# When a gated-convolution group is finished: two completions moved, and one priority kept for a single set of small matmuls

## The chip, the cores and the metric

The kernel runs on one core of a Trainium2 chip. The metric is the device time of one execution in microseconds. Of the kernel before three runs are known, with a median of 897.62 us (896.54 to 897.82). One more execution was profiled; it took 896.51 us, and the times in the tables and rows below are counted from the start of its span of 894.7 us.

The engines are TensorE (PE in the rows; its loads of stationary weights are PEld), VectorE (DVE), ScalarE (ACT), GpSimd (POOL) and SyncE (SP), which issues all DMAs of this kernel from one queue. Each engine works through its own queue in order, and waits where an operand or a buffer is not ready.

## The reference

One decoder layer over 2048 rows of width 1024, all in 32-bit floats, with 16 learned rows put in front:

```python
hn = rms_norm(h, norm_g)
proj = jnp.einsum('bld,de->ble', hn, w_in)
cx, cb, cc, cg, q, k, v, rg = jnp.split(proj, N_PROJ, axis=-1)

u = c_gate * h                        # cc * cx, then 3 causal taps per channel
conv_out = b_gate * conv(u) * jax.nn.silu(cg)

ret = head_group_norm(retention_chunkwise(rotary(q), rotary(k), v), ret_norm_g)
ret_out = ret * jax.nn.silu(rg)

mixed = jnp.concatenate([conv_out, ret_out], axis=-1)
h = h + jnp.einsum('ble,ed->bld', mixed, w_out)
return rms_norm(h, final_g)[:, N_META:]
```

There are four groups of 128 channels of the gated convolution, and four retention heads of 128 channels. A row's norm is a factor per row, so the kernel multiplies the raw x with the weights and scales afterwards: a tile `rr` holds that factor spread over the partitions, `rr2` its square.

## The kernel before, in words

**Two rounds, eight units each.** The rows are cut into two rounds of 1024. In each round eight units are worked through: four heads (units 0 to 3) and four convolution groups (units 4 to 7). `UNITS` (line 36) sets the order: round 0 starts with group 4, the opening group, then the four heads, then groups 5, 6, 7; round 1 takes the heads first and then groups 4 to 7, so that unit 7 is round 1's last group. After the rounds, eight pairs of output rows (2 x 128 rows each) are multiplied with `w_out`, added to x, normalised and stored (`output`, line 692).

**A quad.** The unit of matrix work is `quad` (line 201). It computes two 128-channel projections over 1024 rows as a 2 x 2 block product with seven block products instead of eight. Each block product is 12 matmuls of 128x128 weights by 128x512 columns: four steps over the inner dimension, times three, since each 32-bit operand is split into a rounded half (`wh`, `mh`, a cast on ScalarE, line 101) and a remainder (`wl`, `ml`, a subtraction on VectorE, line 113). So a quad is 84 matmuls, all of line 210. The sums and differences of weight blocks are made on GpSimd (`stationary`, lines 135 to 138), in place, over the blocks as they were loaded. Three buffers each of `wh` and `wl` are there, so the parts of a product can be made up to three products ahead. `quad_plain` (line 249) does the same with eight products from plain blocks (96 matmuls of line 260); the opening group's two quads, round 1's first, and the first pair of output rows use it. Results leave a PSUM bank through a function `take(i, j, bank, copy)`: projection i, half j of the rows.

A head has two quads (K and V, then Q and the gate), and behind them its retention: transposes, state updates, scores, normalisation (lines 616 to 687). A group has two quads as well: `cc` with `cx`, whose product is `u`, and `cg` with `cb`.

**What a group does besides.** `u` is scaled with `rr2`, `carry` (line 447) copies two columns from one half of the rows to the next, `taps` (line 453) makes the three taps (one ScalarE, two VectorE operations for each half). Then the gate `cg` is scaled with `rr` and goes through Silu, the taps are multiplied with `rr`, with the gate and with `cb`, and `store_mixed` (line 440) writes the half to a DRAM tensor `mixed`. There are four of these, one for each 512 rows, and the pairs of output rows read them: pairs 0 and 1 the first, pairs 2 and 3 the second, pairs 4 and 5 the third, pairs 6 and 7 the fourth. What round 1's last group stores is first read by pair 4.

In a normal group (`conv_group`, line 507) the taps come between the two quads, and the second quad's `take` multiplies straight into them (lines 536 to 547): the scaling of the gate on VectorE, Silu on ScalarE, two products on GpSimd, one on VectorE. The opening group (`group_plain`, line 462) copies its results out instead and returns a function `complete`, which does all of the above later. The main loop hands it to the next unit, head 0, as the first member of `between`; `head` (line 565) calls the first member behind its first quad and the second behind its second quad.

**Meta products.** In round 0 each unit's first weight blocks are also multiplied with the 16 learned rows: 32 small matmuls of line 395 (`meta_products`, line 388). They are issued from `ahead` (line 761), at the end of the unit before, and read the blocks as loaded; GpSimd's differences of `stationary`, which overwrite these blocks, wait for them. For the opening group they are issued at line 791, before its quads.

**What sets the order.** The kernel is written on top of a planner. The order of the program gives each instruction its priority; the planner goes through a modelled course of time, and puts into each engine's queue what is ready by its model, of what is ready the earliest in the program. So work of a later place can run before, where an engine is free. `tc.high_priority(offset=HIGH)`, with `HIGH = 400`, gives the instructions in its block the priority of a place 400 instructions earlier. Buffers come from pools with a set number for each tag: 16 of the general kind (`gen`, tag `g`: `u`, copies, taps, x, `w_out`, output rows), 8 raw weight blocks, 4 bank copies (tag `tc`), one rotation table (tag `rot_t`, 128 x 2048 floats).

Of the kernel before, what the change touches and what calls it, by code (L numbers as in the profile page):

```python
# [19 lines left out]
NG = 4  # L20
EPS = 1e-6
HB = 512
NR = 2
BLK = SEQ // NR
# [5 lines left out]
HIGH = 400  # L30
# [40 lines left out]
def hybrid_trunk(ctx: ExitStack, tc: tile.TileContext, t, out: bass.AP, chunk_decay):  # L71
# [5 lines left out]
    nc = tc.nc  # L77
# [307 lines left out]
        nc.vector.tensor_tensor(out=raw, in0=raw, in1=rows, op=ALU.mult)  # L385
        nc.vector.tensor_tensor(out=meta_s, in0=raw, in1=gains, op=ALU.mult)

    def meta_products(blocks):

        bank = ps_misc()  # L390
        four = [bank[i * 32 : i * 32 + NMETA, :P] for i in range(4)]
        with tc.high_priority(offset=HIGH):
            for kt in range(KH):
                for i in (3, 2, 1, 0):
                    nc.tensor.matmul(  # L395
                        four[i], meta_s[:, i % 2 * KH + kt, :], blocks[i][:, kt * P : (kt + 1) * P],
                        start=kt == 0, stop=kt == KH - 1,
                    )
# [41 lines left out]
    def store_mixed(r, j, kt, m):  # L440
        d = mixed[2 * r + j]
        nc.sync.dma_start(
            d[:, :, kt // KH, :, kt % KH, :].rearrange("a i p c -> p a i c"),
            m.rearrange("p (a i c) -> p a i c", a=2, i=2),
        )
# [7 lines left out]
    def taps(u, g):  # L453
        c = gen("c")[:, :HB]
        nc.scalar.mul(c, u[:, 2:], conv_w[:, g, 2:3])
        for tap in (1, 0):
            nc.vector.scalar_tensor_tensor(  # L457
                out=c, in0=u[:, tap : tap + HB], scalar=conv_w[:, g, tap : tap + 1], in1=c, op0=ALU.mult, op1=ALU.add
            )
        return c  # L460

    def group_plain(g, m, f, meta, first, between, ahead):


        u = [gen("u") for _ in range(2)]
        raws = []
        rr, rr2 = ([a[:, j * HB : (j + 1) * HB] for j in range(2)] for a in f[:2])

        def mul(eng, out, a, b):
            eng.tensor_tensor(out=out, in0=a, in1=b, op=ALU.mult)  # L470

        def take(i, j, pp, c):
            s = u[j][:, 2:]
            if i == 0:
                nc.scalar.copy(out=s, in_=pp)
            else:
                mul(nc.vector, s, pp, s)

        quad_plain(first[0], m, take)
        meta_carry(g, meta)  # L480

        def take(i, j, pp, c):
            c = gen("cb")[:, :HB]
            nc.scalar.copy(out=c, in_=pp)
            raws.append(c)

        quad_plain(first[1], m, take)
        between()
        blocks = ahead()

        def complete():
            for j in range(2):
                mul(nc.vector, u[j][:, 2:], u[j][:, 2:], rr2[j])
            carry(u, g, 0)
            for j in range(2):
                gate, other = raws[2 * j : 2 * j + 2]
                c = taps(u[j], g)
                mul(nc.vector, gate, gate, rr[j])
                nc.scalar.activation(gate, gate, AF.Silu)
                mul(nc.gpsimd, c, c, rr[j])  # L500
                mul(nc.vector, c, c, gate)
                mul(nc.vector, c, c, other)
                store_mixed(0, j, g, c)

        return blocks, complete

    def conv_group(g, r, m, f, blocks, ahead):
# [21 lines left out]
        blocks, meta = blocks  # L529
        quad(stationary(blocks), m, take)  # L530
        if meta:
            meta_carry(g, meta)
        carry(u, g, r)
        cs = [taps(u[j], g) for j in range(2)]

        def take(i, j, pp, c):
# [9 lines left out]
                pp = c  # L546
            mul(nc.vector, cs[j], pp, cs[j])

        n = 2 * (NG + g) + 1
        quad(stationary(load_raw(w_loads(n))), m, take)  # L550
        blocks = ahead()
        for j in range(2):
# [218 lines left out]
    for r in range(NR):  # L771
# [113 lines left out]
```

## Time and profile before

| | |
|---|---|
| median of three runs | 897.62 us |
| the profiled execution | 896.51 us |
| its span | 894.7 us |
| TensorE matmuls, busy | 878.3 us (98%) |
| VectorE, busy | 722.4 us (81%) |
| ScalarE, busy | 406.7 us (45%) |
| GpSimd, busy | 403.4 us (45%) |
| opening group's first matmul to head 0's first | 6.3 to 56.6 us |
| head 0's two quads | 56.6 to 98.0 us |
| round 1's last group, second quad | to 733.5 us, its last products mixed with pair 0's first |
| pairs 1, 2, 3, 4 begin | 751.4, 772.7, 791.7, 810.8 us |

How to read the rows that follow. A row of the timeline gives the start and the duration in us, the engine, the line of the kernel, the operation, the tiles (out <- in) and their shapes; `x4` at its end means four alike merged into one row, and brackets hold the idle time ahead of it and what ended it. A row of groups gives the count, then busy time in us and the mean of one in ns. A row of windows gives a stretch, its length, and for PE, PEld, DVE, ACT and POOL the busy time with the number of instructions, then the granted clock, the DMA share and GB/s. A row of the chain that ended last gives start, duration, engine, tile and line. Matmul rows overlap: the next one starts before the one ahead has drained.

### The profile page before, as it was taken

Reading aid. Unit: us, or ns where it says so; the run is one execution under the profiler, and the core shown is the slowest. Engines: PE = TensorE matmul, PEld = TensorE weight load, DVE = VectorE, ACT = ScalarE, POOL = GpSimd, SP = SyncE. Lnnn points to the kernel's source line nnn. Section 1 sums busy time; section 2 is a strip of 40 time slices with the busy share of each in tenths; the row PEclk is TensorE's granted clock in tenths of the full one; section 3 lists DMA queues with packets and bytes.
Section 4 is the critical chain, followed back from the end, with each engine's and each line's share of the span. In section 5 each row is a group of like instructions: output and inputs, shape, how many; then the busy total and the mean of one; then the engine's idle time right before and its main releaser. Section 6 shows DMA issues by size and latency. Waiting matters only on the chain.

```text
span 894.7 us, 12868 instructions
## 1 busy us (share of the span) xinstructions
PE 878.3 (98%) x4407; PEld 726.1 (81%) x4407; DVE 722.4 (81%) x1176; ACT 406.7 (45%) x816; POOL 403.4 (45%) x291
## 2 busy tenths in 40 slices
PE   8999999999999999999999999999999999999996
PEld 6778788888888878788888888888888888788885
DVE  6888878999877867898889899777667698876764
ACT  8763424334245364746243332423433475554553
POOL 0653323322233754452323323354547455777763
PEclk9999999999999999999999999999999999999999
DMA  9711214344224342844135172113221685455432
GB/s 335 249 46 44 76 48 157 127 146 162 61 95 141 92 141 86 296 143 127 52 104 177 57 247 60 59 48 95 69 73 52 210 280 193 159 179 171 171 107 95
DMA packets 76242, 116.94 MB, mean 131 GB/s; under 512 B 7632, under 2 KB 24336, under 8 KB 76176
## 3 DMA queue, kind: packets, MB, share of 16 engines
q1 hardware_dynamic: 76176, 116.11, 40.1%
q8 instruction: 35, 0.57, 0.3%
q14 instruction: 31, 0.25, 0.1%
HBM read 90.92 MB, written 25.17 MB: 130 GB/s over the span
## 4 chain that ended last, share of the span: by engine, by line
PE 80%; DVE 11%; issue 3%; ACT 2%; DMA 2%; POOL 1%; SPq 0%; POOLq 0%; ACTq 0%; DVEq 0%
PE pj L210 62%; PE pj L260 10%; DVE wl L113 2%; PE ms L659 1%; PE ms L660 1%; PE ms L649 1%; PE ms L636 1%; DVE rot L561 1%; DVE ml L113 1%; PE ms L683 1%; PE ms L395 1%; DVE w L113 1%; PE ms L621 1%; DVE x L174 1%; PE ms L626 1%
## 5 line engine op out<-in xcount | busy, mean ns | idle before, releaser
L210 PE MATMUL pj<-mh,wl 128*128 128x512 f32 x1008 | 399.2, 396 | 3.6 <-DVE wl L113 1.5
L210 PE MATMUL pj<-ml,wh 128*128 128x512 f32 x1008 | 394.0, 391 | 0.8 <-DVE ml L113 0.7
L210 PE MATMUL pj<-mh,wh 128*128 128x512 f32 x1008 | 393.7, 391 | 0.0
L101 ACT CAST wh<-ra 128x512 fp32r<-128x512 f32 x216 | 134.0, 621 | 307.6 <-PE pj L210 253.0
L210 PEld LDWEIGHTS pj<-mh,wl 128*128 128x128 f32 x1008 | 189.5, 188 | 46.2 <-ACT tc L217 3.7
L210 PEld LDWEIGHTS pj<-ml,wh 128*128 128x128 f32 x1008 | 189.6, 188 | 39.2 <-DVE ml L113 1.5
L210 PEld LDWEIGHTS pj<-mh,wh 128*128 128x128 f32 x1008 | 189.4, 188 | 39.4
L113 DVE TENSOR_TENSOR wl<-ra,wh 128x512 fp32r<-128x512 f32 x216 | 191.3, 887 | 36.9 <-ACT wh L101 36.3
L113 POOL TENSOR_TENSOR ra<-ra 128x512 f32<-128x512 f32 x72 | 113.6, 1578 | 71.0 <-PE ms L395 35.7
L110 POOL TENSOR_TENSOR sa<-ra 128x512 f32<-128x512 f32 x36 | 57.0, 1584 | 118.5 <-DVE wl L113 48.1
L113 POOL TENSOR_TENSOR ra<-sa,ra 128x512 f32<-128x512 f32 x36 | 52.9, 1471 | 92.0 <-DVE wl L113 91.7
L217 ACT COPY tc<-pj 128x512 f32<-128x512 f32 x108 | 62.6, 579 | 0.0
L260 PE MATMUL pj<-ml,mh 128*128 128x512 f32 x128 | 50.4, 393 | 0.0
L260 PE MATMUL pj<-mh,mh 128*128 128x512 f32 x128 | 50.2, 394 | 0.0
L260 PE MATMUL pj<-mh,ml 128*128 128x512 f32 x128 | 49.0, 399 | 0.1
L672 POOL TENSOR_TENSOR rp<-rs,neg_half 128x4 f32<-128x4 f32 x16 | 19.9, 1245 | 48.3 <-DVE rs L110 48.0
L713 DVE TENSOR_TENSOR yo<-pj,yo 128x512 f32<-128x512 f32 x32 | 22.0, 687 | 18.9 <-POOL yo L110 10.2
L514 POOL TENSOR_TENSOR c<-c,rr 128x512 f32<-128x512 f32 x14 | 26.6, 1900 | 21.3 <-DVE c L457 12.0
L101 ACT CAST wh<-sa 128x512 fp32r<-128x512 f32 x36 | 22.2, 617 | 29.7 <-PE pj L210 29.7
L715 ACT ACTIVATE rot<-yo 128x512 f32<-128x512 f32 x32 | 20.2, 630 | 33.1 <-DVE yo L713 32.7
L514 POOL TENSOR_TENSOR c<-c,tc 128x512 f32<-128x512 f32 x14 | 25.9, 1852 | 19.9 <-ACT tc L540 19.8
L676 DVE TENSOR_SCALAR pm<-ms,mv,rp 128x128 f32<-128x128 f32 x64 | 21.9, 404 | 15.7 <-POOL rp L672 15.7
(135 smaller groups left out, 1159.6 us busy)
## 6 DMA issues: line engine op xcount, KB each, us to landing
ra<-in_w_in SPq DMA_DIRECT2D x128, 256.0 KB, 2.7
x<-in_xT SPq DMA_DIRECT2D x48, 256.0 KB, 5.0
w<-in_w_out SPq DMA_DIRECT2D x32, 256.0 KB, 5.2
ra<-mixed SPq DMA_DIRECT2D x32, 256.0 KB, 2.7
yo<-in_x SPq DMA_DIRECT2D x32, 256.0 KB, 4.4
ra<-in_x SPq DMA_DIRECT2D x16, 256.0 KB, 3.4
mixed<-c SPq DMA_DIRECT2D x16, 256.0 KB, 2.4
mixed<-qg SPq DMA_DIRECT2D x16, 256.0 KB, 2.3
```

The lines of the kernel that those rows point to most:

```text
L101: nc.scalar.copy(out=hi, in_=src)
L110: eng.tensor_tensor(out=out, in0=a, in1=b, op=ALU.add)
L113: eng.tensor_tensor(out=out, in0=a, in1=b, op=ALU.subtract)
L174: nc.vector.scalar_tensor_tensor(out=out, in0=a, scalar=factor, in1=b, op0=ALU.mult, op1=ALU.subtract)
L210: nc.tensor.matmul(bank, a[:, ks], b, start=first and kt == 0 and n == 0, stop=kt == KH - 1 and n == 2, skip_group_check=not first,)
L217: nc.scalar.copy(out=c, in_=bank)
L260: nc.tensor.matmul(banks[i], a[:, ks], b, start=half + kt + n == 0, stop=half == 1 and kt == KH - 1 and n == 2,)
L514: eng.tensor_tensor(out=out, in0=a, in1=b, op=ALU.mult)
L672: nc.gpsimd.tensor_tensor(out=rp, in0=rs, in1=neg_half.rearrange("p (c a) -> p c a", a=1), op=ALU.pow)
L676: nc.vector.tensor_scalar(out=y[:, cs], in0=o[:, cs], scalar1=mv[:, c, 0:1], scalar2=rp[:, c, :], op0=ALU.subtract, op1=ALU.mult,)
L713: last[0] = nc.vector.tensor_tensor(out=y, in0=pp, in1=y, op=ALU.add)
L715: nc.scalar.activation(junk, y, AF.Square, accum_out=ss[:, i, j : j + 1])
```

## The change

Three things are changed. The opening group's `complete` is handed to head 0 as the second member of `between`, with an empty function as the first, so that it stands behind head 0's second quad (Q and gate) instead of its first. Round 1's last group (`following is None and r == NR - 1`) no longer makes its taps between its quads and no longer multiplies in `take`: the second quad's results go into four places of 128x512 in a tile that takes the buffer of the rotation table, and a new function `completion` does the rest; the main loop calls it behind the second pair of output rows (`pair == 1`). `completion` is the second half of the old `complete`, now with the round and the tiles as arguments, and both groups use it. Third, `meta_products` raises its matmuls' priority only where `early` is set, which is so in the opening group's `ahead` (`n == 0`), the set for head 0; in round 1 there are no meta products.

```diff
-    def meta_products(blocks):
+    def meta_products(blocks, early=False):
...
-        with tc.high_priority(offset=HIGH):
+        with tc.high_priority(offset=HIGH) if early else nullcontext():
...
             carry(u, g, 0)
+            completion(g, 0, u, f, raws[0::2], raws[1::2])()
+
+        return blocks, complete
+
+    def completion(g, r, u, f, gates, others):
+
+        rr = [f[0][:, j * HB : (j + 1) * HB] for j in range(2)]
...
+        def complete():
             for j in range(2):
-                gate, other = raws[2 * j : 2 * j + 2]
                 c = taps(u[j], g)
-                mul(nc.vector, gate, gate, rr[j])
-                nc.scalar.activation(gate, gate, AF.Silu)
+                mul(nc.vector, gates[j], gates[j], rr[j])
+                nc.scalar.activation(gates[j], gates[j], AF.Silu)
                 mul(nc.gpsimd, c, c, rr[j])
-                mul(nc.vector, c, c, gate)
-                mul(nc.vector, c, c, other)
-                store_mixed(0, j, g, c)
-
-        return blocks, complete
-
-    def conv_group(g, r, m, f, blocks, ahead):
+                mul(nc.vector, c, c, gates[j])
+                mul(nc.vector, c, c, others[j])
+                store_mixed(r, j, g, c)
+
+        return complete
+
+    def conv_group(g, r, m, f, blocks, ahead, places=None):
...
         carry(u, g, r)
+        n = 2 * (NG + g) + 1
+        if places:
+
+            def take(i, j, pp, c):
+                if c is None:
+                    nc.scalar.copy(out=places[2 * i + j], in_=pp)
+                else:
+                    add(nc.vector, places[2 * i + j], pp, c)
+
+            quad(stationary(load_raw(w_loads(n))), m, take)
+            return completion(g, r, u, f, places[:2], places[2:])
         cs = [taps(u[j], g) for j in range(2)]
...
-    def ahead(r, n):
+    def ahead(r, n, early=False):
...
-        return blocks, meta_products(blocks) if r == 0 else None
+        return blocks, meta_products(blocks, early) if r == 0 else None
...
-            rest = lambda: ahead(r, following)
+            rest = lambda: ahead(r, following, early=n == 0)
...
-                special = (), (complete,)
+                special = (), (lambda: None, complete)
...
+            elif following is None and r == NR - 1:
+                a = sb.tile([P, 2, BLK], F32, name="late", tag="rot_t", bufs=1)
+                complete = conv_group(
+                    unit - NG, r, m, f, blocks, rest, [a[:, i, j * HB : (j + 1) * HB] for i in range(2) for j in range(2)]
+                )
...
         output(pair, m, final_g)
+        if pair == 1:
+            complete()
```

More of the change, by code (lines that the diff above doesn't have):

```diff
@@ L466, in group_plain @@
         raws = []
-        rr, rr2 = ([a[:, j * HB : (j + 1) * HB] for j in range(2)] for a in f[:2])
+        rr2 = [f[1][:, j * HB : (j + 1) * HB] for j in range(2)]
         def mul(eng, out, a, b):
@@ L494, in complete, with mul @@
             carry(u, g, 0)
+            completion(g, 0, u, f, raws[0::2], raws[1::2])()
+        return blocks, complete
+    def completion(g, r, u, f, gates, others):
+        rr = [f[0][:, j * HB : (j + 1) * HB] for j in range(2)]
+        def mul(eng, out, a, b):
+            eng.tensor_tensor(out=out, in0=a, in1=b, op=ALU.mult)
+        def complete():
             for j in range(2):
-                gate, other = raws[2 * j : 2 * j + 2]
                 c = taps(u[j], g)
-                mul(nc.vector, gate, gate, rr[j])
-                nc.scalar.activation(gate, gate, AF.Silu)
+                mul(nc.vector, gates[j], gates[j], rr[j])
+                nc.scalar.activation(gates[j], gates[j], AF.Silu)
                 mul(nc.gpsimd, c, c, rr[j])
-                mul(nc.vector, c, c, gate)
-                mul(nc.vector, c, c, other)
-                store_mixed(0, j, g, c)
-        return blocks, complete
-    def conv_group(g, r, m, f, blocks, ahead):
+                mul(nc.vector, c, c, gates[j])
[3 more added lines that the diff above has]
+    def conv_group(g, r, m, f, blocks, ahead, places=None):
         u = [gen("u") for _ in range(2)]
@@ L547, in take @@
             mul(nc.vector, cs[j], pp, cs[j])
-        n = 2 * (NG + g) + 1
         quad(stationary(load_raw(w_loads(n))), m, take)
```

## The prediction

> **What bounds the kernel now.** I read the page first, then the waits of TensorE, then the chain that ended last, then the timeline of each engine around the places that the change touches.
>
> ```profile
> span 894.7 us, 12868 instructions
> PE 878.3 (98%) x4407; PEld 726.1 (81%) x4407; DVE 722.4 (81%) x1176; ACT 406.7 (45%) x816; POOL 403.4 (45%) x291
> PEclk9999999999999999999999999999999999999999
> ```
>
> TensorE is at work 98% of the span at full clock. How full it is within that shows in the chain:
>
> ```profile
> 607.03 103.42 PE pj L210 x456
> ```
>
> 456 matmuls in 103.42 us, one every 0.227 us, back to back. Where the matmuls follow at that rate, nothing on another engine matters. What can be won is only the gaps, and the waits of PE (microseconds, times, longest) list them:
>
> ```profile
> PE ms L659 <- DVE pm L651: 2.3, 2, 1.2
> PE pj L210 <- DVE wl L113: 1.5, 2, 1.0
> PE pj L210 <- ACT tc L217: 1.3, 2, 0.7
> PE pj L210 <- DVE ml L113: 0.7, 1, 0.7
> PE pj L210 <- DVE qg L110: 0.6, 1, 0.6
> ```
>
> These five rows hold 6.4 us, nearly all that matmuls wait for other engines once the start is over. They are too short as printed, because a matmul's printed time overlaps the next one. So I take each gap from start to start, less 0.227.
>
> **The opening group's completion.** Behind head 0's first quad it issues eight VectorE operations that touch the taps: four taps (L457), two products with the gate and two with the other projection (L470, four together), with two products on GpSimd. The row scalings, the Silu and the copy of the carry ran earlier, whenever engines were free; I leave these where they are. The view of groups in the stretch 77 to 98 us prices the eight, and the timeline shows where they stand:
>
> ```profile
> L457 DVE SCALAR_TENSOR_TENSOR c<-u,conv_w,c 128x512 f32<-128x512 f32 x4 | 3.8, 1002 | 0.0
> L470 DVE TENSOR_TENSOR c<-c,cb 128x512 f32<-128x512 f32 x4 | 3.7, 954 | 0.0
> ```
>
> ```profile
> 77.25 1.34 ACT L455 ACTIVATE c<-u,conv_w 128x512 f32<-128x512 f32 x2
> 85.11 0.62 ACT L101 CAST wh<-ra 128x512 fp32r<-128x512 f32 x1 [2.28 <-PE pj L210]
> 90.81 0.68 DVE L113 TENSOR_TENSOR wl<-ra,wh 128x512 fp32r<-128x512 f32 x1
> 90.30 0.39 PE L210 MATMUL pj<-mh,wh 128*128 128x512 f32 x1
> 91.64 0.47 PE L210 MATMUL pj<-mh,wl 128*128 128x512 f32 x1 [0.96 <-DVE wl L113]
> 94.26 0.39 PE L210 MATMUL pj<-mh,wh 128*128 128x512 f32 x1
> 95.23 0.50 PE L210 MATMUL pj<-mh,wl 128*128 128x512 f32 x1 [0.58 <-DVE qg L110]
> 88.18 3.11 SPq L442 DMA_DIRECT2D mixed<-c  x2
> 91.35 0.49 SPq L413 DMA_DIRECT2D mr<-in_rot_m  x1
> 94.02 0.35 DVE L418 TENSOR_TENSOR mk<-mk,mr 16x64 f32<-16x64 f32 x2 [0.72 <-DMA mr<-in_rot_m]
> ```
>
> The weights' remainder at 90.81 had its rounded half ready at 85.7; it stood 5 us behind products of the completion, and TensorE lost 91.64 - 90.30 - 0.23 = 1.11. The second gap, 95.23 - 94.26 - 0.23 = 0.74, goes through the SP queue: the two stores wait for c until 90.9, the load of mr behind them goes out at 91.35, VectorE waits for it at 94.02, and the addition that frees the bank comes after. With the completion behind the second quad, the remainder stands ahead of the eight and mr ahead of the stores. Both gaps go: **-1.85**, between -1.85 and 0 (0 if the planner runs the eight as early as before; against that, the taps begin at 77.25, when the first quad is over, though their operands were ready before).
>
> What is late next: the eight now compete with head 0's retention and head 1's first quad.
>
> ```profile
> 98.00:118.00 20.00, 20.00 (x138) 17.04 (x137) 16.14 (x26) 9.71 (x24) 7.63 (x5) 1.00 0.15 44
> 113.02 0.69 DVE L113 TENSOR_TENSOR wl<-ra,wh 128x512 fp32r<-128x512 f32 x1
> 114.78 3.19 PE pj L210 x14
> ```
>
> (In the windows the third busy figure is VectorE, the fifth GpSimd.) VectorE is busy 16.14 of 20.00 us there, so 3.86 are free. The eight cost 8 x 0.7 = 5.6 at the least and 7.5 at the row's price. They overrun by 1.7 to 3.6. The remainder at 113.02 is done at 113.7 and its product starts at 114.78: a reserve of 1.1. So 0.6 to 2.5 us are lost, or nothing if retention's matmuls are put in between. I take the row's lower end: **+0.6**, between 0 and +2.5. The two stores pass to the SP queue behind the loads of head 1's first quad; what is queued behind them there are loads of its second quad, 20 us from use: 0, and up to the 0.74 of the old gap if one of them is needed at once.
>
> **The last group's completion.** From the stretch 711 to 751 us go four taps, two row scalings and two products on VectorE, and four products on GpSimd; one bank copy comes to ScalarE (0.58 us). Three additions remain, now into the places.
>
> ```profile
> 711.00:724.00 13.00, 13.00 (x58) 10.47 (x56) 12.98 (x21) 12.29 (x24) 7.07 (x4) 1.00 0.82 269
> 751.00:772.70 21.70, 20.24 (x85) 15.41 (x84) 18.46 (x25) 12.88 (x26) 13.21 (x11) 1.00 0.75 244
> 772.70:791.70 19.00, 19.00 (x85) 15.77 (x84) 16.12 (x18) 10.65 (x24) 16.66 (x12) 1.00 0.52 168
> 791.70:810.80 19.10, 19.10 (x85) 15.79 (x85) 11.74 (x19) 9.79 (x20) 13.28 (x11) 1.00 0.54 175
> 723.64 0.39 PE L210 MATMUL pj<-mh,wh 128*128 128x512 f32 x1
> 724.09 0.50 PE L260 MATMUL pj<-mh,ml 128*128 128x512 f32 x1
> ```
>
> VectorE is full from 711 to 724 (12.98 of 13.00), yet TensorE loses only 724.09 - 723.64 - 0.23 = 0.22 there. That goes: **-0.22**, between -0.22 and 0. The larger gaps come one pair later:
>
> ```profile
> 762.10 0.39 PE L210 MATMUL pj<-mh,wh 128*128 128x512 f32 x1
> 763.06 0.47 PE L210 MATMUL pj<-mh,wl 128*128 128x512 f32 x1 [0.57 <-DVE wl L113]
> ...
> 750.95 1.37 DVE L713 TENSOR_TENSOR yo<-pj,yo 128x512 f32<-128x512 f32 x2 [2.93 <-PE pj L260]
> 754.58 0.72 ACT L737 ACTIVATE z<-z,rf 128x512 f32<-128x512 f32 x1 [1.37 <-POOL rf L276]
> ```
>
> The gap at 763.06 is 0.73, printed as 0.57. In the whole stretch of 751 to 772.7 TensorE is idle 21.70 - 20.24 = 1.46 as printed, so some 2 us. Here VectorE has been idle (2.93 us before 750.95), so its earlier load is not the cause. The casts of the eight stored sums stand in ScalarE's order behind pair 0's scaling at 754.58, and their remainders then meet pair 1's weights. The change moves none of that. I take **0**, between -2.0 (the planner sets the casts earlier, since VectorE is free sooner) and +0.7 (row scalings and Silu slip in between).
>
> Behind pair 1 come ten VectorE operations (the products with the gate move from GpSimd to VectorE), two GpSimd products, four ScalarE operations and two stores. Ten at 0.68 us (the remainder alone, above) to 1.15 (remainders in that stretch, where GpSimd works beside them):
>
> ```profile
> L113 DVE TENSOR_TENSOR wl<-ra,wh 128x512 fp32r<-128x512 f32 x13 | 14.9, 1150 | 3.2 <-ACT wh L101 3.1
> ```
>
> make 6.8 to 11.5 us. VectorE has 2.9 us free in pair 2 (19.00 - 16.12) and 7.4 in pair 3 (19.10 - 11.74). Pair 4 starts at 810.8 and is the first to read these stores; its loads wait for them in the SP queue, and behind those loads the rows of x and the stores of pairs 2 and 3. If the ten are done within pair 2, by 791.7, a whole pair is left for the stores, the loads and the first casts: 0; if not, what is late then is pair 4's first product. Until then the taps push weights' remainders back. A remainder can wait two products, 24 x 0.227 = 5.4, less cast and remainder (0.62, 0.69): 4.1 us. They are spread over two pairs by their waits on GpSimd, so I take a gap of the size that a full VectorE left at 724, 0.22: **+0.2**, between 0 and +4.5 (worked out below).
>
> The places take the buffer of the rotation table, free since round 1's last head: 0. Of the 16 general buffers the two of the group's products stay taken until the completion is over, and it takes two more. Twelve are left, and two pairs in flight hold 2 x (4 rows of x + 2 products) = 12, so 0. Where one is short, a load of x is late:
>
> ```profile
> yo<-in_x SPq DMA_DIRECT2D x32, 256.0 KB, 4.4
> ```
>
> 4.4 us to landing less the two products that a bank can wait, 5.4, is still 0.
>
> [...]
>
> **The priority.** Of eight sets of 32 small matmuls only the one for head 0 keeps it. The first set comes ahead of its quad in the program anyway; six are free to move.
>
> ```profile
> 291.42 1.00 PE ms L395 x32
> 331.89 1.28 POOL L113 TENSOR_TENSOR ra<-ra 128x512 f32<-128x512 f32 x1
> 338.40 1.59 POOL L113 TENSOR_TENSOR ra<-sa,ra 128x512 f32<-128x512 f32 x1 [2.95 <-DVE wl L113]
> ```
>
> 1.00 us a set, wherever it stands. Later means that GpSimd's differences, which overwrite the blocks they read, start later. At the end of a quad, two products (5.4 us) cover 1.28 + 1.59 + 0.62 + 0.69 = 4.2. A reserve of 1.2 remains: **0**. No wait of TensorE is behind these sets, so a gain is excluded; the bound above is two conv products on GpSimd ahead of the differences, 2 x 1.3 - 1.2 = 1.4 us a group, +2.8 for the last two.
>
> **The sum**, against the profiled execution's own 896.51 us: -1.85 + 0.6 - 0.22 + 0.2 = -1.3, so 895.2. The median of the runs, 897.62, stands 1.11 above that execution, so **896.3** (the rivals' times below are of that median).
>
> [...]
>
> **Rivals.** (1) Nothing comes back: retention's matmuls and pair 3's idle time take in both completions. For: 7.4 us of VectorE are free in pair 3. -1.85 - 0.22 = -2.1: 895.5. (1b) As well, the gaps of pair 1 close: -4.1, 893.5. Against: ScalarE's order. (2) Slower: the ten operations are served ahead of pair 2's remainders, because their place in the program is before them. At 1.15 us they overrun pair 2's 2.9 by 8.6; less the 4.1 that a remainder can wait, TensorE loses 4.5. It decides from 7.0 us of completion within pair 2. -1.85 + 0.6 - 0.22 + 4.5 = +3.0: 900.6. Against: they are spread by waits on GpSimd. (3) The small matmuls come too late in the conv groups: -1.3 + 2.8 = +1.5, 899.1. Against: the reserve of 1.2 us. (4) The planner fills idle slots as before and nothing moves: 897.6.
>
> **Chances.** Forecast 0.36, (1) 0.25, (1b) 0.11, (2) 0.15, (3) 0.07, (4) 0.06. A measurement here tells about 0.2%, 1.8 us. Rivals (1) and (1b) are beyond it on the fast side, 0.36. The forecast and (4) lie within, 0.42. Rivals (2) and (3), 0.22, count as slower; (3) at 1.5 us lies just short of the bound, but its second term may be met with a part of (2). The forecast's own range is 895.8 to 898.5. The range 893.0 to 900.2 leaves out the far halves of (1b) and (2).
>
> **What would show it.** Right: no gap at 90 to 95; mr loaded before the stores of the opening group; a new gap below 1 us between 100 and 118; gaps of pair 1 about 2 us still; ten completion operations spread over pairs 1 to 3, both stores out before pair 3 is over. Wrong: gaps above 1 us in pairs 2 or 3 or a wait for a load of pair 4; the small matmuls right at the end of a quad with a gap at the third product after it; the taps of the opening group still ahead of 95.

## The result and the profile after

The changed kernel takes 908.68 us (median of five runs, 906.26 to 909.92), the kernel before 897.62 us in the same session. The ratio is 1.0128, with a 95% interval of 1.0109 to 1.0147: slower by 11 us, where the prediction said 896.3 and a range up to 900.2. The profiled execution of the changed kernel took 909.7 us, 13.2 more than the one of before.

The first rows of the page after:

```profile
span 907.9 us, 12867 instructions
PE 886.7 (98%) x4407; PEld 729.4 (80%) x4407; DVE 715.6 (79%) x1178; ACT 408.0 (45%) x817; POOL 396.2 (44%) x289
PEclk9999989999999999999999999999999999999999
```

TensorE does the same 4407 matmuls, and its busy time has grown from 878.3 to 886.7 us all the same: most of that growth isn't waiting. The clock row gives a hint of it, an 8 in the sixth slice (113 to 136 us), where before has only nines.

Where the 13.2 us lie follows from the start of the same instruction in both traces:

| stretch of the changed kernel | difference |
|---|---|
| start to head 0's transposes (98.1 us) | -1.5 |
| to the first transpose of head 0's normalised output (131.9 us) | +6.4 |
| heads 1 and 2 | -1.5 |
| head 3 and the conv groups of round 0, to 344.9 us | +2.6 |
| round 1 | -0.7 |
| the pairs of output rows, to the end | +8.0 |

The gain that was forecast came: no gap at 90 to 95 us. It is lost four times over right behind. The waits of TensorE after (total us, times, longest us):

```profile
PE pj L210 <- DVE wl L113: 4.3, 2, 2.7
PE ms L681 <- DVE pm L673: 3.3, 1, 3.3
```

The two rows stand for two places. At the first, TensorE waits for the masked scores of head 0's first half, pm. VectorE's timeline ahead of it (start us, duration us) and the group of taps in 98 to 117 us:

```profile
107.55 3.47 DVE L504 TENSOR_TENSOR c<-c,cb 128x512 f32<-128x512 f32 x2 [1.19 <-POOL c L504]
110.94 0.68 DVE L110 TENSOR_TENSOR kv<-pj,tc 128x512 f32<-128x512 f32 x1
111.54 1.16 DVE L504 TENSOR_TENSOR c<-c,cb 128x512 f32<-128x512 f32 x1
114.96 0.69 DVE L504 TENSOR_TENSOR c<-c,cb 128x512 f32<-128x512 f32 x1
119.00 0.74 DVE L673 SCALAR_TENSOR_TENSOR pm<-ms,cols,causal 128x512 f32<-128x512 f32 x1
```

```profile
L457 DVE SCALAR_TENSOR_TENSOR c<-u,conv_w,c 128x512 f32<-128x512 f32 x4 | 4.9, 1255 | 0.0
```

Four taps of 4.9 us in all and four products of 5.3 (3.47 + 1.16 + 0.69) stand ahead of pm (the four row scalings ran before 60 us), and VectorE waits 1.19 us for GpSimd's product besides. Before, pm was made at 114.82; now it starts at 119.00. TensorE's timeline at that place, and the same stretch in windows of 3.41 us (the first busy figure is TensorE; the granted clock stands behind the five busy figures):

```profile
116.08 0.39 PE L210 MATMUL pj<-mh,wh 128*128 128x512 f32 x1
119.80 0.80 PE L681 MATMUL ms<-kv,pm 128*128 128x128 f32 x2 [3.33 <-DVE pm L673]
...
123.80 0.63 PE L210 MATMUL pj<-ml,wh 128*128 128x512 f32 x1
124.23 0.63 PE L210 MATMUL pj<-mh,wh 128*128 128x512 f32 x1
...
126.04 0.39 PE L210 MATMUL pj<-ml,wh 128*128 128x512 f32 x1
126.27 0.39 PE L210 MATMUL pj<-mh,wh 128*128 128x512 f32 x1
```

```profile
115.42:118.83 3.41, 1.04 (x5) 0.53 (x3) 3.24 (x10) 0.62 (x1) 0.00 (x0) 1.00 0.42 98
118.83:122.24 3.41, 2.44 (x11) 2.44 (x12) 2.91 (x6) 0.00 (x0) 0.80 (x1) 0.50 0.37 99
122.24:125.66 3.42, 3.42 (x13) 2.94 (x12) 1.33 (x9) 0.00 (x0) 1.86 (x2) 0.50 0.12 44
```

The gap is 119.80 - 116.08 - 0.23 = 3.5 us. Then the price is paid a second time: the clock stands at 0.50 for two such windows, and the matmuls follow each other every 0.43 us (123.80 to 124.23) instead of 0.23 (126.04 to 126.27). From 119.80 to 125.66 TensorE runs at half speed, which costs half of 5.86, 2.9 us. Gap and halved clock make the +6.4.

The second place is pair 2, where eight of the last group's ten VectorE instructions stand, the taps and the four products. (The two row scalings ran at 723.40 and 740.75 us, in round 1's last stretch.) TensorE's waits there, and the two remainders of weights that it waits for, with the casts on ScalarE that had made them ready:

```profile
790.88 0.39 PE L210 MATMUL pj<-mh,wh 128*128 128x512 f32 x1
792.84 0.47 PE L210 MATMUL pj<-mh,wl 128*128 128x512 f32 x1 [1.58 <-DVE wl L113]
...
795.46 0.39 PE L210 MATMUL pj<-mh,wh 128*128 128x512 f32 x1
798.52 0.77 PE L210 MATMUL pj<-mh,wl 128*128 128x512 f32 x1 [2.67 <-DVE wl L113]
```

```profile
786.78 0.61 ACT L101 CAST wh<-ra 128x512 fp32r<-128x512 f32 x1
793.77 0.60 ACT L101 CAST wh<-ra 128x512 fp32r<-128x512 f32 x1
```

```profile
787.02 1.78 DVE L504 TENSOR_TENSOR c<-c,late 128x512 f32<-128x512 f32 x1
789.39 1.62 DVE L504 TENSOR_TENSOR c<-c,late 128x512 f32<-128x512 f32 x1
791.00 1.70 DVE L113 TENSOR_TENSOR wl<-ra,wh 128x512 fp32r<-128x512 f32 x1
794.93 1.77 DVE L504 TENSOR_TENSOR c<-c,late 128x512 f32<-128x512 f32 x1
796.62 1.75 DVE L113 TENSOR_TENSOR wl<-ra,wh 128x512 fp32r<-128x512 f32 x1
```

The first remainder could have started at 787.4, stands behind two products of the completion and starts at 791.00; the second could have started at 794.4, finds a product of the completion ahead of it and starts at 796.62. From start to start the gaps are 1.74 and 2.83, with a first one of 0.62 at 784.70: 5.2 us. Here too the clock is halved behind a gap:

```profile
770.83:774.24 3.41, 3.41 (x10) 2.65 (x9) 2.56 (x5) 0.72 (x2) 0.77 (x1) 0.51 0.32 77
798.13:801.54 3.41, 3.02 (x7) 2.48 (x8) 2.70 (x5) 0.72 (x2) 1.22 (x1) 0.51 0.74 215
```

Half of the time that TensorE works in these two windows (3.41 and 3.02 us) is lost, 1.7 and 1.5 us, the first behind pair 1's gaps, which the kernel before has too. 5.2 + 3.2 = 8.4, less a little that pair 1's gaps shrank, is the +8.0. VectorE has indeed got its relief at 711 to 751 us (8.7 us idle ahead of 756, and the gap of 0.22 at 724 is gone), at a place where it was worth nothing more.

### The profile page after: what moved, and what is told of

Its sections match the earlier page's. It is cut to its first block, busy times and chain, and to the rows that moved or that the text cites. A ratio compares the mean times of both kernels' runs of the same rounds, so it can differ in the third digit from the quotient of the medians.

```text
span 907.9 us, 12867 instructions
## 1 busy us (share of the span) xinstructions
PE 886.7 (98%) x4407; PEld 729.4 (80%) x4407; DVE 715.6 (79%) x1178; ACT 408.0 (45%) x817; POOL 396.2 (44%) x289
## 4 chain that ended last, share of the span: by engine, by line
PE 80%; DVE 8%; ACT 2%; issue 1%; DMA 1%; POOL 1%; SPq 0%; POOLq 0%; ACTq 0%; DVEq 0%
PE pj L210 66%; PE pj L260 5%; PE ms L681 2%; DVE wl L113 2%; PE ms L682 1%; PE ms L671 1%; PE ms L658 1%; DVE c L504 1%; DVE c L457 1%; PE ms L395 1%; PE ms L705 1%; PE ms L643 1%; PE ms L648 1%; DVE w L113 1%; DMA x<-in_xT 1%
## 5 line engine op out<-in xcount | busy, mean ns | idle before, releaser
L113 DVE TENSOR_TENSOR wl<-ra,wh 128x512 fp32r<-128x512 f32 x216 | 188.6, 874 | 39.1 <-ACT wh L101 38.6
L113 POOL TENSOR_TENSOR ra<-ra 128x512 f32<-128x512 f32 x72 | 115.7, 1608 | 92.2 <-issue 34.3
L113 POOL TENSOR_TENSOR ra<-sa,ra 128x512 f32<-128x512 f32 x36 | 50.9, 1414 | 92.0 <-DVE wl L113 88.2
L110 POOL TENSOR_TENSOR yo<-yo,tc 128x512 f32<-128x512 f32 x21 | 32.6, 1560 | 6.1 <-ACT tc L217 4.8
L113 DVE TENSOR_TENSOR ml<-t,mh 128x512 fp32r<-128x512 f32 x40 | 34.2, 898 | 0.8 <-ACT mh L101 0.8
```

Source lines behind the costliest of these rows:

```text
L110: eng.tensor_tensor(out=out, in0=a, in1=b, op=ALU.add)
L113: eng.tensor_tensor(out=out, in0=a, in1=b, op=ALU.subtract)
```

## The experiments

Three theories stood at the start. Q: VectorE serves the completions in program order, ahead of what TensorE needs, and the halved clock comes on top. P: the priority sets off the gap at 116. S: the gaps need all parts of the change together. All ratios are to the kernel before in the same session (897.93, 897.59 and 898.28 us in the three).

**The opening group alone.**

```diff
-                special = (), (complete,)
+                special = (), (lambda: None, complete)
```

> The kernel before with only the opening group's completion moved behind head 0's second quad. Theory Q (the completion's operations stand in VectorE's queue ahead of what TensorE waits for): the gaps at 90 to 95 us go (-1.9 us), a gap of about 3.5 us stands before the first score product of head 0 (near 116 us), and TensorE's clock is halved behind it for 3.4 or 6.8 us; in all +3.5 to +5 us (ratio 1.004 to 1.006). Theory P (the small matmuls without priority delay head 0's retention): no gap near 116 us, in all -1.9 us. Theory S (the parts hurt only together): within 1 us of before.

900.89 us, ratio 1.0030 (1.0016 to 1.0044). The gaps at 90 to 95 are gone, the gap ahead of pm is there with nothing else changed, and so is the halved clock (a window, columns as above):

```profile
118.50:125.30 6.80, 5.24 (x20) 4.90 (x21) 4.77 (x17) 0.00 (x0) 2.07 (x2) 0.50 0.29 82
```

P and S fall. Its ten runs go from 897.81 us at a mean granted clock of 0.998 to 903.23 at 0.992, and the profiled one, at 0.992, took 902.55: the longer runs have the lower clocks. Only one of the ten has a trace, so where the clock went down in the others isn't shown. In that trace the clock is halved at pair 1 as well (770.4 us), behind gaps that the kernel before has too; that costs 1.2 us there.

**The last group alone** (the opening group and the priority as before).

```diff
+                complete = conv_group(
+                    unit - NG, r, m, f, blocks, rest, [a[:, i, j * HB : (j + 1) * HB] for i in range(2) for j in range(2)]
+                )
...
+        if pair == 1:
+            complete()
```

> The kernel before with only the last group's completion deferred behind pair 1. Theory Q: gaps of 0.5 to 3 us in pair 2 before products whose weight remainder stands behind the taps and products in VectorE's queue, and a halved clock after the longest; +6 to +8.5 us in all (ratio 1.007 to 1.0095). Theory P or S: under +2 us. If buffers (two more held) were the cause, the gaps would stand before waits for loads of x instead.

902.75 us, ratio 1.0061 (1.0041 to 1.0081). Gaps of 1.24, 1.75 and 2.83 us in pair 2, 5.8 in all, but here without a halved clock:

```profile
792.93 0.47 PE L210 MATMUL pj<-mh,wl 128*128 128x512 f32 x1 [2.66 <-DVE wl L113]
793.24 0.40 PE L210 MATMUL pj<-ml,wh 128*128 128x512 f32 x1
793.47 0.39 PE L210 MATMUL pj<-mh,wh 128*128 128x512 f32 x1
```

The same wait as at 798.52 in the changed kernel (2.67 us), and the matmuls behind it follow every 0.23 us, not every 0.43.

**The priority alone.**

```diff
-        with tc.high_priority(offset=HIGH):
+        with tc.high_priority(offset=HIGH) if early else nullcontext():
```

> The kernel before with only the priority of the small matmuls changed. Theory Q: a set is split in two around a product (some +0.3 us a set, 6 sets), groups 6 and 7 lose about 1 us each, and the gaps of 1.3 us in heads 1 and 2 go; 0 to +2 us in all (ratio 1.000 to 1.002), no halved clock. Theory P: the gap near 116 us is here, +5 us or more. Theory S: within 1 us of before.

898.88 us, ratio 1.0011 (0.9997 to 1.0025): not told apart from no change. In its trace the two gaps of 1.3 us at heads 1 and 2 are gone (-1.5 us), and +2.6 us come by the end of round 0's conv groups, with a gap of 0.7 at 307 us; the sets of 32 small matmuls run in pieces. These are the -1.5 and the +2.6 of the changed kernel. A gap of 1.3 us at 725 us is there too, but it isn't the priority's: it stands at the same matmul in opening_gpsimd and before_gpsimd, whose priority is as before.

**The opening group's products on GpSimd**, moved as in opening_only.

```diff
-                mul(nc.vector, c, c, gate)
-                mul(nc.vector, c, c, other)
+                mul(nc.gpsimd, c, c, gate)
+                mul(nc.gpsimd, c, c, other)
```

> As opening_only, but the opening group's four products with the gate and with the other projection run on GpSimd, which idles for 9 us there in the changed kernel. Theory Q: VectorE is relieved by 4 operations (2.7 to 5 us), the gap near 116 us falls below 1 us, no halved clock, and the time is 1 to 2 us below before (ratio 0.998 to 0.999). [...]

898.26 us, ratio 1.0005 (0.9994 to 1.0015): the loss of opening_only is gone. pm comes at 117.79 us, and TensorE's gap is 118.59 - 116.47 - 0.23 = 1.9 us, with no halved clock behind it (the matmuls of pm and the states behind follow every 0.23 us):

```profile
116.47 0.39 PE L210 MATMUL pj<-mh,wh 128*128 128x512 f32 x1
118.59 0.49 PE L659 MATMUL ms<-kv,pm 128*128 128x128 f32 x2 [1.72 <-DVE pm L651]
118.91 0.39 PE L660 MATMUL ms<-state,qg 128*128 128x128 f32 x2
```

Four of eight instructions less on VectorE halve the gap. The gap of 1.9 and the -1.85 that the move brings cancel.

**The gap filled with idle matmuls**, on top of opening_only.

```diff
             o = ps_misc()
+            for _ in range(16 if r + h + j == 0 else 0):
+                nc.tensor.matmul(
+                    o.rearrange("p (a c) -> p a c", a=CH), warm,
+                    warm.rearrange("p (a c) -> p a c", a=1).broadcast_to([P, CH, P]), start=True, stop=True,
+                )
```

> The opening group's completion is moved as in opening_only (900.9 us; the gap of 3.7 us ahead of head 0's first output product is followed by 6.83 us at a granted clock of 0.50), and 16 idle bf16 matmuls are put on TensorE behind head 0's first score products, into the bank that those output products then overwrite; one of them lasts about 0.22 us at the full clock, so that they fill 3.5 us, about the length of the gap. Theory H (the gap costs its own length and then a second price, the halved clock, because TensorE stood still): no stretch at 0.50 near 118, no gap above 1 us there, and a time 2 to 3 us below opening_only's, 898 to 899. Rival (the halved clock has another cause, or costs nothing because VectorE is what is late): the stretch at 0.50 stays, or goes without the time moving: 900.5 to 901.5.

901.91 us (899.01 to 902.83), ratio 1.0039 (1.0021 to 1.0056). Half of theory H came: the profiled execution has no stretch at 0.50 between the start and the last matmul, and a mean clock of 0.998 (opening_only's had 0.992).

```profile
112.30 3.62 PE L658 MATMUL ms<-warm 128*128 128x512 bf16 x16
115.56 0.58 PE L210 MATMUL pj<-ml,wh 128*128 128x512 f32 x1
...
119.21 0.49 PE L664 MATMUL ms<-kv,pm 128*128 128x128 f32 x2 [1.68 <-DVE pm L651]
```

That execution took 899.5 us, 3.0 less than opening_only's profiled one; the median over all runs did not fall. Counted between the same matmuls, only 0.8 of the 3.0 lie between the transposes and the outputs of head 0, where the fillers are; 1.2 lie at pair 1, where opening_only's execution had its clock halved. The planner put the fillers ahead of the projection's matmuls and six of those behind pm, so that a wait of 1.68 us stayed and TensorE's order changed as well: the fillers took the time that the gap and the halved clock had taken. This kernel doesn't show that the halved clock is what can be saved. That the clock goes down for want of matmuls agrees with its one trace, but the gap is shorter there too (1.9 us in place of 3.7).

**The opening group's completion behind head 0**, its VectorE instructions held behind head 0's second pm.

```diff
-                special = (), (complete,)
+                special = (), ()
...
+                if r + unit == 0:
+                    with tc.issue_after(pms[1].ins):
+                        complete()
```

> The opening group's completion, with its first four products, is called behind the whole of head 0, and its VectorE instructions are put behind head 0's second masking of the scores (pm). Theory Q (the cost of the move was the place in VectorE's order, ahead of pm): the gaps at 90 to 95 us stay away (-1.85 us against before), the gap at 116 is below 0.7 us, no halved clock, 896 to 897 us. Rival (the ten instructions stall TensorE wherever they are put in heads 0 and 1, because VectorE has no room of 16 us there): a gap of 2 us or more stands between 118 and 145 us, and the time is 898 to 901 us.

903.09 us, ratio 1.0061 (1.0045 to 1.0078). The rival held, and by more than its own time. No gap is left at 116, but between 123 and 166 us there are six, from 0.6 to 2.0 us by the starts, and behind the last of 2.0 the clock is halved for 3.41 us (148.5). The longest two by the trace's own count:

```profile
127.84 0.50 PE L210 MATMUL pj<-mh,wl 128*128 128x512 f32 x1 [1.61 <-DVE kv L110]
...
147.90 0.50 PE L210 MATMUL pj<-mh,wl 128*128 128x512 f32 x1 [1.86 <-DVE qg L110]
```

So pm isn't the only wrong neighbour. But this kernel moves more than opening_only does: the hold also keeps back the four row scalings, which ran before 60 us there and run from 124.05 to 126.53 here, so that twelve VectorE instructions stand behind pm, not the ten that were expected and not opening_only's eight. In the kernel before, VectorE is idle for 3.65 of the 22 us from 118 to 140 and for 1.98 of the 26 us from 140 to 166; twelve at 0.68 us are 8.2, more than that. Whether the eight alone would have fitted there isn't shown.

**The last group's completion emptied.**

```diff
             for j in range(2):
+                if r:
+                    store_mixed(r, j, g, gates[j])
+                    continue
                 c = taps(u[j], g)
```

> As last_only (902.75 us), but the last group's completion leaves its computation out: no filter, no products, it only stores the two held tiles, so that the second half of group 3's output isn't computed. What is kept is the other side of the move: the two held tiles, their place in the buffers, the stores behind the second pair. Theory Q (ten VectorE instructions stand ahead of pair 2's remainders): the gaps of 1.24, 1.75 and 2.83 us at 778 to 790 us vanish, and the time is 896.5 to 898 us. Rival R (buffers held longer, or the stores, delay pair 2's loads): gaps of 3 us or more in all stay there, 900.5 to 903 us.

896.94 us, ratio 0.9996 (0.9987 to 1.0006). The gaps of pair 2 are gone; of the waits for remainders only those of pair 1 are left:

```profile
PE pj L210 <- DVE wl L113: 1.5, 2, 0.9
```

The held tile and the late stores cost nothing, as the prediction had it. The loss comes with the completion's own instructions. One thing isn't tested here: without the taps, the two buffers of the group's products aren't held and none are taken for the taps. In last_only's trace, though, neither TensorE nor the casts of weights wait for a load in pair 2. The run also says what could be won at most by taking this work out of the stretch 711 to 751: nothing that can be measured.

**The last group's four products on GpSimd.**

```diff
-                mul(nc.vector, c, c, gates[j])
-                mul(nc.vector, c, c, others[j])
+                mul(nc.gpsimd if r else nc.vector, c, c, gates[j])
+                mul(nc.gpsimd if r else nc.vector, c, c, others[j])
```

> As last_only (902.75 us), but the four products of the last group's completion with the gate and the other tile are made on GpSimd; the filter's four instructions and the two gate products stay on VectorE. Theory Q: VectorE is relieved of four of ten instructions, about 6.5 of some 16 us; what remains shifts pair 2's remainders by about half as much, so that the gaps of 5.8 us fall to 1 to 3 us and the time to 898.5 to 900.5 us. Rival K (what VectorE loses is time beside GpSimd, not its own instructions): GpSimd's four products slow VectorE's neighbours, the gaps stay at 4 us or more, 901.5 to 903.5 us.

906.02 us, ratio 1.0087 (1.0065 to 1.0109): worse than last_only, and outside both expectations. Gaps of 1.25, 1.16, 1.79 and 2.13 us stand at 780, 787, 794 and 812, with a halved clock of 3.41 us at 816. GpSimd's timeline and VectorE behind it:

```profile
790.32 2.99 POOL L504 TENSOR_TENSOR c<-c,late 128x512 f32<-128x512 f32 x2
793.28 1.71 POOL L113 TENSOR_TENSOR ra<-ra 128x512 f32<-128x512 f32 x1
794.95 2.98 POOL L110 TENSOR_TENSOR yo<-yo,tc 128x512 f32<-128x512 f32 x2
```

```profile
796.72 0.69 DVE L735 TENSOR_TENSOR yo<-pj,yo 128x512 f32<-128x512 f32 x1 [1.18 <-POOL yo L110]
```

In the pairs GpSimd has the differences of the weight blocks and the additions to y to do, and the products now stand ahead of them; VectorE, which was to be relieved, waits for GpSimd. Rival K's reason (slow neighbours) isn't needed for that. At the opening group, moved, the same exchange helped; in the changed kernel GpSimd has nothing to do for 8.9 us ahead of 121. That it is idle isn't enough, as the last run below shows.

**The last group's completion one pair later.**

```diff
-        if pair == 1:
+        if pair == 2:
```

> As last_only (902.75 us), the last group's completion behind the third pair of output rows in place of the second. Theory Q (ten VectorE instructions stand ahead of the next pair's remainders, wherever that is): the gaps leave 778 to 790 us and stand at 797 to 812 us, again 4.5 to 6.5 us in all, and since the next pair loads what is stored here, up to 2 us more: 901.5 to 905 us. Rival (pair 2 is a narrow place of its own, right behind the work that the block change leaves): gaps of 2 us or less, 898.5 to 900.5 us.

901.07 us, ratio 1.0034 (1.0021 to 1.0047), between the two expectations. The gaps move along, as Q has it, but they are two of 1.33 and 1.77 us, each below the rival's 2, and 3.1 in place of 5.8:

```profile
799.12 0.50 PE L210 MATMUL pj<-mh,wl 128*128 128x512 f32 x1 [1.17 <-DVE rs_v L273]
...
806.48 0.50 PE L210 MATMUL pj<-mh,wl 128*128 128x512 f32 x1 [1.61 <-ACT tc L217]
```

Pair 3 has more room than pair 2, as the busy times before had said, not enough of it.

**Both moves, without the priority's change.**

```diff
-        with tc.high_priority(offset=HIGH) if early else nullcontext():
+        with tc.high_priority(offset=HIGH):
```

> Both completions are moved as in the changed kernel, all products of meta keep their priority. Theory A (the parts add up, and what the changed kernel lost beyond their sum is the clock halved three times, 1.7 to 2.9 us each, after the gaps of both moves): opening_only's +3.0 and last_only's +4.8 over 897.9 make 905.7, and up to 2 us more where the clock is halved behind pair 1 or 2 as well: 905 to 908 us, with stretches at a granted clock of 0.50 behind the gaps. Rival (the excess comes from the priority together with the moves): 903 to 905.5 us, and no stretch at 0.50 behind 760 us.

908.47 us, ratio 1.0115 (1.0101 to 1.0128): all of the changed kernel's loss without the priority. The product of the two single ratios, 1.0030 x 1.0061 = 1.0091, is 2.1 us short of it. Theory A's stretch at half clock behind pair 2 is there (the time lies 0.5 us above A's range):

```profile
794.10:797.60 3.50, 0.82 (x4) 0.67 (x4) 3.50 (x4) 0.62 (x1) 2.05 (x2) 0.99 0.43 150
797.60:801.00 3.40, 3.40 (x9) 2.65 (x8) 1.56 (x3) 0.72 (x2) 2.36 (x2) 0.50 0.93 252
```

TensorE works through all of its 3.40 us at half speed, which costs 1.7. Over pair 2 this execution loses 7.8 us, last_only's 6.2, with the same gaps. Its four runs had mean clocks of 0.993 to 0.995, those of last_only 0.997 to 0.998; opening_only's, with the opening group's move alone, go from 0.992 to 0.998, so the means don't tell the second stretch from the first. That the excess over the sum is this clock, the profile bears out in size; no run took the one without the other.

**The opening group and the priority together.**

```diff
-                special = (), (complete,)
+                special = (), (lambda: None, complete)
...
+        with tc.high_priority(offset=HIGH) if early else nullcontext():
```

> The changed kernel without the last group's move. Theory A (the parts add up): opening_only's +3.0 and priority_only's +1.0 over 897.9 make 901.9; range 900.5 to 903 us, the gap at 116 at 3.5 us with the halved clock behind it. Rival (the priority's loss came from a gap of the opening group that the move takes away, or the gaps of 1.3 us at heads 1 and 2 that the priority takes away come to bear): 898.5 to 900.3 us.

902.87 us, ratio 1.0049 (1.0031 to 1.0067), additive within the intervals (1.0030 x 1.0011 = 1.0041). The gap ahead of pm is 3.5 us, the halved clock behind it there; the mean clock of the profiled execution is 0.994.

**The kernel before with the opening group's products on GpSimd**, nothing moved.

```diff
-                mul(nc.vector, c, c, gate)
-                mul(nc.vector, c, c, other)
+                mul(nc.gpsimd, c, c, gate)
+                mul(nc.gpsimd, c, c, other)
```

> The kernel before with nothing moved, but the opening group's four products with the gate and the other tile made on GpSimd. Theory Q (VectorE's order in front of TensorE's remainders is what costs): VectorE is relieved of four products of 0.7 to 1.8 us between 86 and 98 us, the gaps of 1.1 and 0.8 us at 91 and 95 us shrink, and the time is 895.8 to 897.0 us. Rival (GpSimd's products come out late and slow, as in last_gpsimd, and push back its own cast and sum work): gaps stay or new ones stand at 95 to 120 us, 897.5 to 900 us.

899.63 us, ratio 1.0016 (1.0007 to 1.0026): slower, the rival. The gaps at 91 and 95 have become one of 2.5 us, again with the clock halved behind it (0.50 from 92.96 to 96.38). TensorE and VectorE there:

```profile
90.16 0.39 PE L210 MATMUL pj<-mh,wh 128*128 128x512 f32 x1
92.89 0.70 PE L210 MATMUL pj<-mh,wl 128*128 128x512 f32 x1 [2.34 <-DVE wl L113]
```

```profile
87.69 1.68 DVE L561 TENSOR_TENSOR rot<-qg,rot_t 64x512 f32<-64x512 f32 x1
89.40 1.67 DVE L562 TENSOR_TENSOR qg<-qg,rot_t 128x512 f32<-128x512 f32 x1
91.00 1.75 DVE L113 TENSOR_TENSOR wl<-ra,wh 128x512 fp32r<-128x512 f32 x1
```

VectorE has four products less to do, and each of the five instructions that it starts between 86.01 and 92.67 us takes 1.67 to 1.76 us, while GpSimd is at work without a break from 85.38 to 93.88. The next one, at 94.35, is of the same line and shape as the one at 91.00 and takes 0.68 in place of 1.75.

GpSimd had been idle at this place, too. In the kernel before:

```profile
99.83 1.28 POOL L113 TENSOR_TENSOR ra<-ra 128x512 f32<-128x512 f32 x1 [12.83 <-PE ms L395]
```

So an idle GpSimd doesn't make the exchange a gain by itself: moved behind the second quad it took 2.6 us off opening_only's time, and here it cost some 1.4.

No kernel tried here beats the kernel before by more than can be measured.

## Why the prediction was wrong

**The opening group's gaps, -1.85: right.** They are gone in every kernel that moves the completion behind the second quad.

**The gap that reappears, +0.6: the first step that failed; it measured +6.4** in the changed kernel's trace (4.9 by opening_only's median, 3.0 + 1.85). It failed three times. The row was sought in the wrong place: the reserve of 1.1 us was worked out for a weights' remainder, and the instruction that came late first is pm, on which the next matmuls in TensorE's order depend. (The reserve was misread as well. Counted in twelves from head 1's first matmul at 100.48, the products start at 115.08 and 119.51, none at 114.78; with the remainders taken in their order, the one of 113.02 belongs to 119.51, a reserve of 5.8.) "Retention's matmuls put in between" was to be the relief; they are what waits. The instructions were too cheap: eight at 0.7 to 0.94 us, 5.6 to 7.5 in all, and they took 4.9 + 5.3 = 10.2, with 1.2 more of waiting for GpSimd; GpSimd worked beside most of them, on its two products and on weight blocks, from 98.3 to 112.2. pm came 4.2 us later. And a gap of 3.5 us then brought 2.9 us of halved clock, of which there is no term in the sum.

**The gap at 724, -0.22: right** against the trace of before. Its size varies, though: in four of the kernels that leave the last group in its place (priority_only, opening_priority, opening_gpsimd, before_gpsimd) the gap at this matmul is 1.3 us. Why isn't shown.

**Pair 1's gaps, 0: right** for the gaps themselves; in the changed kernel the clock was halved once behind them (1.7 us).

**The last group behind pair 1, +0.2: the second step that failed; alone it measured 4.8 us, in the changed kernel 8.0.** Rival (2) has the mechanism and the place: operations served ahead of pair 2's remainders. The argument against it, that waits on GpSimd spread the ten over two pairs, is what failed: all that came behind pair 1 are served from 779.8 to 796.7 us. They are eight, not ten, since the row scalings ran early, as the opening group's do; and the eight took 9.8 us, 1.2 each, more than the row's 1.15. That rival (2)'s 4.5 us for the move alone comes so near is therefore in part luck. The bound of 7.0 us from which it was to decide holds: 9.8 us of completion lie above it, and TensorE lost time. last_bare confirms two steps put at nothing, the held tile and the stores; the general buffers it doesn't test.

**The priority, 0: not told apart from 0** (alone +1.0, 0.9997 to 1.0025; taken out of the changed kernel, 908.47 against 908.68). In the trace of the changed kernel +2.6 in head 3 and round 0's conv groups stand against -1.5 at heads 1 and 2, where two gaps of 1.3 us are gone, and priority_only's trace has the same two figures: the term is a loss and a gain, +1.1 in all. "A gain is excluded" was wrong; the two gaps stand in the prediction's own first row of waits (pm, 2.3 us).

**The range** ended at rival (2)'s 900.6, with one mechanism at a time. The two moves failed together, and the halved clock had no rival: between the start and the last matmul it is in no row of before, where the longest gap is 1.3 us.

## What to carry to other kernels

Where TensorE is full, work that is moved on VectorE should be fitted to the next thing that TensorE needs from VectorE, whatever it is, at the price that the instruction has beside a busy GpSimd (in before_gpsimd a remainder took 1.75 us there and 0.68 behind it); an average of free time over 20 us says little. Relief counts only at a pinch: the stretch with VectorE at 12.98 of 13.00 us had a gap of 0.22. And some gaps on TensorE cost half as much again, or nearly double, by the clock: in the changed kernel one of 2.83 us brought 1.5 more and one of 3.5 us 2.9 more, while one of 2.83 us in last_only brought nothing more. The mean clocks of one kernel's runs differ (0.992 to 0.998 in opening_only), so the total of one trace is read beside the medians.

## What the runs showed of the hardware

The clock is halved in stretches of 3.41 us, or twice that, and whether a gap of one length brings it differs: 2.67 us did at 798 in the changed kernel, 2.66 didn't in last_only. The records show a pattern. In the changed kernel's trace the clock changes at 118.83, 125.66, 770.78, 774.19, 798.09 and 801.50 us: 2, 189, 1, 7 and 1 times 3.413 us apart. If time is cut into stretches of that length that join at the clock's last change in each trace, and TensorE's idle time is counted in each (from start to start, less 0.227 us a projection matmul and 0.11 a matmul of 128x128), then in the changed kernel three stretches at full clock hold more than 2 us of idle time, 2.53 from 115.42, 2.14 from 767.37 and 2.40 from 794.67, and each is followed by a stretch at 0.50. The next seven of the changed kernel and of the kernel before hold 1.00 to 1.90 us, and none of them is. Counted so in all fourteen profiled executions (from 20 us on, to the last matmul), of the 12 stretches at full clock with 1.98 us or more 11 are followed by a stretch at 0.50; the other one had 2.0. None of the some 70 with 1.0 to 1.96 us is. Within a halved clock it is otherwise: three halved stretches with 1.0 to 1.7 us of idle time, counted at the halved rate, are followed by a second one (1.12 from 118.83 in the changed kernel), and the others, with 0.6 or less, aren't (0.12, 0.00 and 0.54 in the changed kernel). The two gaps of 2.7 us differ in how a border cuts them:

| execution | stretch from us | idle us | clock behind |
|---|---|---|---|
| changed kernel | 794.7 | 2.40 | 0.50 |
| last_only | 787.9 and 791.3 | 1.19 and 1.72 | 1.00 |
| changed kernel, pair 1's gaps | 767.4 | 2.14 | 0.50 |
| before, the same gaps | 762.6 | 1.90 | 1.00 |

So in these traces a gap above 2 us cost 1.5 to 2.9 us more, or nothing, and where the borders fall is the one difference seen between the two of 2.7. This was read from the traces afterwards, and the border near 2 us was set with them; no kernel was made to test it. A stretch need not be idle throughout: from 115.42 to 118.83, ahead of the halved clock, TensorE was busy for 1.04 of 3.41 us.
